# An encoder layer's state-space phase as a software pipeline with TensorE's order written out

## The chip, the cores and the metric

The kernel runs on one core of a Trainium2 chip. The metric is the device time of one launch in microseconds (us), taken as the median of several runs. In the profile PE is TensorE (matmuls), PEld its weight loads, DVE VectorE, ACT ScalarE, POOL GpSimd, SP SyncE (which here only starts transfers).

## The reference

One layer of a hybrid encoder in fp32 over 1024 tokens of width 1024, followed by cross-attention into 256 memory rows and a squared-ReLU MLP. What matters here is the first sublayer, the state-space branch above all:

```python
h = rmsnorm(x, norm_mix); proj = h @ w_in                   # q, k, v, z, xBC, dt, two gates
attn = windowed_gqa_sink(q, k, v, sink)                     # 16 heads, 4 kv heads, |t-s| <= 128
xbc = silu(depthwise_conv_centred(xbc, conv_w, conv_b))     # 5 taps; 2048 x, 1024 B, 1024 C
dt  = softplus(dt_raw + dt_bias)                            # per direction and head
# per direction (the backward one on flipped tokens), per group of 4 heads, chunks of 128 tokens:
#   CB     = C @ B.T;  Wd = CB * exp(masked difference of cumulated dt*A)
#   y_diag = Wd @ (x*dt);  states = B.T @ (decay * x*dt)
#   prev   = running sum of states over the chunks, decayed
#   y_off  = (C @ prev) * exp(cumulated dt*A)
y = (y_fwd + y_bwd + d_skip * x) * silu(z); y = grouped_rmsnorm(y) * norm_g
merged = sigmoid(gate_a) * (attn @ w_attn_branch) + sigmoid(gate_b) * (y @ w_ssd_branch)
x = x + merged @ w_out                                      # then cross-attention, then the MLP
```

## The kernel before

Every matmul with a weight is done on exact high and low halves, in three matmuls (`mm3`, L79 on). A weight block of 128x1024 comes by SP's queue into one of 2 `raw` buffers, ScalarE makes its high half (`whi`, L67), GpSimd its low half (`wlo`, L68), in one of 3 slots. All activations of the layer stand in `hT` (in the trace `kt`), feature by feature, two halves of 512 tokens.

The phases follow each other: norms, memory keys and values and the decay sums of dt (`phase0`, `dt_part`, tiles `dtt`, `r`, `acc`, `e`), then `ssd_phase`, `attn_phase` (4 key/value heads), `merge_cross_phase`, `mlp_phase`.

`ssd_phase` loops over 8 groups. For a group: four conv tiles (two of x, tile `cx`; B, tile `cB`; C, tile `cC`), each 48 matmuls of 128x512 into a psum tile `cps` and then one ScalarE and four VectorE products for the five taps, a tanh and a product; transposes into token-major `xtok` and `btok` (`tm`); eight states (`st`, from `xs` = x times decay, and `btok`) and their running sum `prev`; the z projection, 192 matmuls of 128x256 (`zp`), into `zs`; the scan of eight chunks from the last to the first: rows of the cumulated decay loaded by ScalarE's queue, exponents `ef` and `eb`, `cb` = C @ B.T, the product of both with `xtok` (written `cb` too, L427), `yo` = C @ prev, the sum `y` in `yz`, its square sum; after each half of the chunks the scaling, the transposes `yt`, their eviction into `yts` and a store to `d_y`. Behind each group stands one gate tile of 48 matmuls (`gps`; two behind the last), its tanh `gt` stored for the merge. Attention has one gate tile behind each key/value head, the merge three at its start; their first matmuls are pinned in program order.

Nothing sets the order inside the phases but the scheduler: it lists each engine's instructions by its own estimates, within what buffers allow. psum is split into `pg` (2 tiles of 128x1024, for `cps` and `gps`) and `pp` (4 tiles of 128x512 for all else). The gates are dealt out by three tables:

```python
SSD_GATES = ((0,), (1,), (2,), (3,), (4,), (5,), (6,), (7, 8))
ATT_GATES = ((9,), (10,), (11,), (12,))
END_GATES = (13, 14, 15)
```

Of the kernel before, what the change touches and what calls it, by code (L numbers as in the profile page):

```python
# [60 lines left out]
def split_in(kx, src, hi, lo, eng=None):  # L61
    """Load src and split it: hi + lo == src exactly."""
    nc = kx.nc
    n = hi.shape[-1]
    raw = kx.wp.tile([P, 1024], F32, tag="raw", bufs=kx.raw_bufs, name="raw")[:, :n]
    nc.sync.dma_start(raw, src)
    nc.scalar.activation(hi, raw, AF.Copy)  # L67
    (eng or nc.gpsimd).tensor_tensor(lo, raw, hi.bitcast(F32), ALU.subtract)  # L68
# [10 lines left out]
def mm3(kx, out, l, r, first, last):  # L79
    """out += l.T @ r with l, r given as exact (hi, lo) pairs."""  # L80
    mm = kx.nc.tensor.matmul
    i = mm(out, l[0], r[0], start=first, stop=False)  # L82
# [3 lines left out]
    mm(out, l[0], r[1], start=False, stop=False)  # L86
    mm(out, l[1], r[0], start=False, stop=last)  # L87
# [17 lines left out]
def gemm_fm(kx, ps, w, act, first=True, last=True):  # L105
    """feature-major GEMM over one half of the tokens: ps = w.T @ act"""
# [25 lines left out]
def norm_tile(kx, pool, xt, xn, grow, dst, off):  # L132
    """RMSNorm of 128 rows, transposed and split into dst at token offset off."""
# [77 lines left out]
def dt_part(kx, ins, dr, p0):  # L211
    """Softplus of dt, the decay sums and their layouts; rows are (direction, half, head)."""
# [99 lines left out]
def ssd_phase(kx, ins, dr):  # L312
    nc, tc = kx.nc, kx.tc
    V, A, G, PE = nc.vector, nc.scalar, nc.gpsimd, nc.tensor
    with tc.tile_pool(name="p1", bufs=1) as sp:
# [4 lines left out]
        def conv_tile(g, i, tag, bufs):  # L320
            w = wload(kx, ins["wssd"][g, i])
            ps = kx.pg.tile([P, S], F32, tag="g", name="cps")
            for h in range(2):
                gemm_fm(kx, ps[:, h * 512:(h + 1) * 512], w, kx.hT[h])
            j = 4 * g + i
            cw = lambda k: kx.cw[:, 5 * j + k:5 * j + k + 1]
            acc = ca.tile([P, S], F32, tag=tag, bufs=bufs, name=tag)
# [7 lines left out]
            th = ca.tile([P, S], F32, tag="tab", bufs=1, name="th")  # L335
            A.activation(th, acc, AF.Tanh)
            V.scalar_tensor_tensor(acc, th, 1.0, acc, ALU.add, ALU.mult)
            return acc
# [9 lines left out]
        for g in range(NG):  # L348
            xtok = ca.tile([P, NT, 256], F32, tag="xtok", bufs=1, name="xtok")
            btok = ca.tile([P, NT, P], F32, tag="btok", bufs=1, name="btok")  # L350
            for i in range(2):
                tok_major(conv_tile(g, i, "cx", 2), xtok[:, :, i * P:(i + 1) * P])
            BT = conv_tile(g, 2, "cB", 2)
            tok_major(BT, btok)
            CT = conv_tile(g, 3, "cC", 1)

            hs = slice(4 * g, 4 * g + 4)
            prev = sp.tile([P, NT, 2, 256], F32, tag="prev", bufs=1, name="prev")

            def decay(d, c):  # L360
                o = 64 * d + 32 * (c // 4) + 4 * g
                return kx.dec[:, o:o + 4, c % 4:c % 4 + 1].broadcast_to([P, 4, 64])

            def heads(ap):
                return ap.rearrange("p (h q) -> p h q", h=4)

            for c in range(NT):
                xs = sp.tile([P, 2, 4, 64], F32, tag="xs", bufs=2, name="xs")
                V.tensor_tensor(xs, heads(xtok[:, c]).unsqueeze(1).broadcast_to([P, 2, 4, 64]),
                                kx.coef[:, c // 4, c % 4, :, hs].unsqueeze(3).broadcast_to([P, 2, 4, 64]), ALU.mult)  # L370
                lo, hi = (256 if c == NT - 1 else 0), (256 if c == 0 else 512)
                st = kx.pp.tile([P, 512], F32, tag="p", name="st")
                PE.matmul(st[:, lo:hi], btok[:, c], xs.rearrange("p d h q -> p (d h q)")[:, lo:hi],  # L373
                          start=True, stop=True)
                if c == 0:
                    A.activation(prev[:, 1, 0], st[:, :256], AF.Copy)
                elif c < NT - 1:
                    V.tensor_tensor(heads(prev[:, c + 1, 0]), heads(prev[:, c, 0]), decay(0, c), ALU.mult)
                    V.tensor_tensor(prev[:, c + 1, 0], prev[:, c + 1, 0], st[:, :256], ALU.add)
                if c > 0:  # L380
                    A.activation(prev[:, c - 1, 1], st[:, 256:], AF.Copy)
            for c in range(NT - 2, 0, -1):
                t = sp.tile([P, 256], F32, tag="p1", bufs=2, name="cb_t")
                G.tensor_tensor(heads(t), heads(prev[:, c, 1]), decay(1, c), ALU.mult)
                G.tensor_tensor(prev[:, c - 1, 1], prev[:, c - 1, 1], t, ALU.add)

            zhl = [sp.tile([P, 1024], F32R, tag=f"z{i}", bufs=1, name=f"z{i}") for i in range(2)]
            zw = [wload(kx, ins["wssd"][g, 4], hi=zhl[0], lo=zhl[1]), wload(kx, ins["wssd"][g, 5])]
            zws = wsplit(zw[0], 4) + wsplit(zw[1], 4)
            zs = sp.tile([P, NT, 256], F32, tag="zs", bufs=1, name="zs")  # L390
            for b in range(3, -1, -1):
                zp = kx.pp.tile([P, 512], F32, tag="p", name="zp")
                for j in range(2):
                    t = 2 * b + j
                    for k in range(NK):
                        mm3(kx, zp[:, j * 256:(j + 1) * 256],
                            act_pair(kx.hT[t // 4], k, slice((t % 4) * P, (t % 4) * P + P)),
                            zws[k], k == 0, k == NK - 1)
                zb = zs[:, 2 * b:2 * b + 2].rearrange("p c q -> p (c q)")
                A.activation(zb, zp, AF.Tanh, scale=0.5)  # L400
                V.scalar_tensor_tensor(zb, zb, 1.0, zp, ALU.add, ALU.mult)

            for b in (1, 0):
                yz = sp.tile([P, 4, 256], F32, tag="yz", bufs=1, name="yz")
                ss = sp.tile([P, 4], F32, tag="ss", bufs=2, name="ss")
                for j in range(3, -1, -1):
                    c = 4 * b + j
                    cl = slice(c * P, (c + 1) * P)
                    rows = sp.tile([P, 2, 4, P], F32, tag="rows", bufs=2, name="rows")
                    for d in range(2):  # L410
                        o = 64 * d + 32 * b + 4 * g
                        nc.scalar.dma_start(rows[:, d], dr.cs[o:o + 4, j * P:(j + 1) * P].partition_broadcast(P))
                    G.affine_select(out=rows[:, 0], in_=rows[:, 0], compare_op=ALU.is_ge, fill=NEG, base=0,
                                    pattern=[[0, 4], [1, P]], channel_multiplier=-1)
# [10 lines left out]
                    V.tensor_tensor(ef, ef, cb[:, :P].unsqueeze(1).broadcast_to([P, 4, P]), ALU.mult)
                    for h in range(4):
                        PE.matmul(cb[:, 256 + 64 * h:256 + 64 * h + 64], ef[:, h], xtok[:, c, 64 * h:64 * h + 64],  # L427
                                  start=True, stop=True)
                    lo, hi = (256 if c == 0 else 0), (256 if c == NT - 1 else 512)
                    yo = kx.pp.tile([P, 512], F32, tag="p", name="yo")  # L430
                    PE.matmul(yo[:, lo:hi], CT[:, cl], prev[:, c].rearrange("p d q -> p (d q)")[:, lo:hi],
                              start=True, stop=True)
                    d0, d1 = lo // 256, hi // 256
                    t = sp.tile([P, 2, 256], F32, tag="t", bufs=1, name="t")
# [23 lines left out]
            for m in SSD_GATES[g]:  # L458
                gate_block(kx, ins, dr, m, ca)
# [509 lines left out]
```

## Time and profile before

| what | us |
|---|---|
| median of 3 runs | 2534.68 (2529.97 to 2538.14) |
| profiled execution, its span | 2540.5 (no time of its own beside the span is given) |
| TensorE busy | 2446.7 |
| phase 0 | 0 to 59.9 |
| state-space phase | 59.9 to 979.9 |
| attention | 980 to about 1319 |
| merge and cross-attention | to about 1500 |
| MLP | to the end |

Rows of waits read "engine, waiting tile and line <- engine, tile and line waited for: total, times, longest". Rows of a timeline give start, length, engine, line, operation, tiles, shape and count, and in brackets the idle time before with what ended it. Rows of windows give the stretch, its length, and then busy time and instructions of PE, PEld, DVE, ACT and POOL, the granted clock of TensorE, the share of the DMA engines and GB/s.

### The profile page before, as it was taken

How to read it: one execution, taken by the hardware profiler on the slowest of the kernel's cores; microseconds unless marked ns; L12 is line 12 of the kernel's file. 1: busy time of each engine (PE TensorE's matmuls, PEld its weight loads, DVE VectorE, ACT ScalarE, POOL GpSimd, SP SyncE). 2: the span in 40 equal slices, each digit the busy share in tenths (PEclk: the TensorE clock that was granted, in tenths of full speed). 3: DMA queues.
4: the chain of work that ended last, by engine and by line, in shares of the span. 5: the costliest groups of instructions: out<-in, count | busy, mean ns of one | idle time of the engine just before them, and what ended most of it. 6: DMA issues, size and time to landing. Idle time of an engine off the chain costs nothing.

```text
span 2540.5 us, 32272 instructions
## 1 busy us (share of the span) xinstructions
PE 2446.7 (96%) x12348; PEld 2014.4 (79%) x12348; DVE 1286.9 (51%) x2033; ACT 1030.6 (41%) x2114; POOL 936.2 (37%) x808
## 2 busy tenths in 40 slices
PE   7899999999999999999999999999999999999998
PEld 6677877777787778777778878888988888888887
DVE  5856556565755655465553342335543434343435
ACT  5445436363544534576773232235432121212112
POOL 4253434344344433444454444224332131312120
PEclk9999999999999999999999999999999999999999
DMA  6223223131313312111125454412121121111111
GB/s 221 75 71 104 92 59 117 52 123 46 112 63 88 108 44 90 48 48 46 50 90 201 134 206 129 170 50 67 59 75 67 34 67 34 66 34 58 42 34 67
DMA packets 135914, 212.20 MB, mean 84 GB/s; under 512 B 9680, under 2 KB 84560, under 8 KB 135760
## 3 DMA queue, kind: packets, MB, share of 16 engines
q1 hardware_dynamic: 58528, 159.80, 18.9%
q10 hardware_dynamic: 77232, 50.35, 6.7%
q8 instruction: 97, 1.59, 0.3%
q14 instruction: 57, 0.47, 0.1%
HBM read 183.63 MB, written 26.48 MB: 83 GB/s over the span
## 4 chain that ended last, share of the span: by engine, by line
PE 71%; DVE 12%; ACT 6%; POOL 4%; DMA 3%; issue 3%; ACTq 0%; POOLq 0%; SPq 0%; DVEq 0%
PE dps L87 4%; PE dps L86 4%; PE dps L82 4%; PE ups L82 4%; PE ups L86 4%; PE ups L87 4%; PE mps L87 3%; PE mps L82 3%; PE mps L86 3%; PE zp L82 2%; PE zp L87 2%; PE zp L86 2%; DMA rows<-d_cs 2%; PE st L373 2%; PE gps L82 2%
## 5 line engine op out<-in xcount | busy, mean ns | idle before, releaser
L68 POOL TENSOR_TENSOR wlo<-raw,whi 128x1024 fp32r<-128x1024 f32 x170 | 416.6, 2452 | 570.4 <-ACT whi L67 556.4
L67 ACT ACTIVATE whi<-raw 128x1024 fp32r<-128x1024 f32 x172 | 181.8, 1057 | 365.0 <-PE mps L86 111.7
L850 DVE TENSOR_TENSOR x<-x,dps 128x512 f32<-128x512 f32 x256 | 175.6, 686 | 124.9 <-PE dps L87 123.2
L68 POOL TENSOR_TENSOR wdl<-raw,wdh 128x1024 fp32r<-128x1024 f32 x32 | 76.0, 2396 | 423.2 <-ACT wdh L67 423.2
L82 PE MATMUL cps<-kt,whi 128*128 128x512 f32 x512 | 203.0, 396 | 6.9 <-DVE cx L334 6.9
L86 PE MATMUL cps<-kt,whi 128*128 128x512 f32 x512 | 203.8, 398 | 0.0
L87 PE MATMUL cps<-kt,wlo 128*128 128x512 f32 x512 | 201.4, 393 | 0.0
L82 PE MATMUL ups<-kt,whi 128*128 128x512 f32 x512 | 199.7, 390 | 0.2
L86 PE MATMUL ups<-kt,whi 128*128 128x512 f32 x512 | 199.4, 390 | 0.0
L87 PE MATMUL ups<-kt,wlo 128*128 128x512 f32 x512 | 199.2, 389 | 0.0
L86 PE MATMUL dps<-wdl,u 128*128 128x512 f32 x512 | 199.2, 389 | 0.0
L87 PE MATMUL dps<-wdh,u 128*128 128x512 f32 x512 | 199.2, 389 | 0.0
L82 PE MATMUL dps<-wdh,u 128*128 128x512 f32 x512 | 199.2, 389 | 0.0
L824 DVE TENSOR_TENSOR u<-ups,ru 128x512 f32<-128x512 f32 x64 | 44.1, 689 | 256.5 <-ACT ru L822 254.3
L67 ACT ACTIVATE wdh<-raw 128x1024 fp32r<-128x1024 f32 x32 | 32.3, 1053 | 229.9 <-PE dps L87 229.7
L82 PEld LDWEIGHTS cps<-kt,whi 128*128 128x128 f32 x512 | 96.6, 189 | 27.1 <-issue 7.7
L82 PEld LDWEIGHTS ups<-kt,whi 128*128 128x128 f32 x512 | 96.1, 188 | 20.7 <-DVE u L824 0.6
L86 PEld LDWEIGHTS ups<-kt,whi 128*128 128x128 f32 x512 | 96.1, 188 | 20.0 <-DVE kt L145 0.2
L87 PEld LDWEIGHTS ups<-kt,wlo 128*128 128x128 f32 x512 | 96.1, 188 | 20.0
L87 PEld LDWEIGHTS dps<-wdh,u 128*128 128x128 f32 x512 | 96.1, 188 | 20.0
L82 PEld LDWEIGHTS dps<-wdh,u 128*128 128x128 f32 x512 | 96.1, 188 | 20.0
L86 PEld LDWEIGHTS dps<-wdl,u 128*128 128x128 f32 x512 | 96.1, 188 | 19.9
(311 smaller groups left out, 6460.2 us busy)
## 6 DMA issues: line engine op xcount, KB each, us to landing
rows<-d_cs ACTq DMA_DIRECT2D x128, 256.0 KB, 3.8
raw<-in_wssd_dram SPq DMA_DIRECT2D x48, 512.0 KB, 3.9
raw<-in_wsb_dram SPq DMA_DIRECT2D x32, 512.0 KB, 3.3
raw<-in_wup_dram SPq DMA_DIRECT2D x32, 512.0 KB, 3.2
raw<-in_wdn_dram SPq DMA_DIRECT2D x32, 512.0 KB, 3.2
x<-in_x_dram SPq DMA_DIRECT2D x16, 512.0 KB, 7.7
raw<-in_wg_dram SPq DMA_DIRECT2D x16, 512.0 KB, 3.9
raw<-in_wa_dram SPq DMA_DIRECT2D x16, 512.0 KB, 3.3
```

Source lines behind the costliest of these rows:

```text
L67: nc.scalar.activation(hi, raw, AF.Copy)
L68: (eng or nc.gpsimd).tensor_tensor(lo, raw, hi.bitcast(F32), ALU.subtract)
L82: i = mm(out, l[0], r[0], start=first, stop=False)
L86: mm(out, l[0], r[1], start=False, stop=False)
L87: mm(out, l[1], r[0], start=False, stop=last)
L373: PE.matmul(st[:, lo:hi], btok[:, c], xs.rearrange("p d h q -> p (d h q)")[:, lo:hi], start=True, stop=True)
L824: V.tensor_tensor(u2, pv, r, ALU.mult)
L850: V.tensor_tensor(xh, xh, ps, ALU.add)
```

## The change

`ssd_phase` is written as a list of jobs, under a manual schedule for TensorE: in it TensorE's instructions run in the order of the code; the other engines stay with the scheduler. A job loads the next job's weights, then runs its matmuls in chunks of three (one `mm3`), and after given chunks other work is dealt in. For group g the jobs are conv 0, conv 1, gate g, conv 2, conv 3, z. The scan steps of group g−1 stand after chunks 8 and 16 of the first four; a step issues the next chunk's loads, exponents and `cb` (`prep`), then its own products. The group's states stand after every eighth chunk of z. In group 0 conv 0 and conv 1 alternate by halves, and nothing is dealt into them. At the end gates 8, 9 and 10 take the last group's steps. So 11 gates stand in the phase, three in attention (none for the last key/value head), two in the merge. Buffers: `cB` 2 to 1, `tab` (tanh and gate) 1 to 2, `yz` one of 128x4x256 to six of 128x256; the square goes into `zs`. Gate and y stores go on SP's queue.

```diff
-SSD_GATES = ((0,), (1,), (2,), (3,), (4,), (5,), (6,), (7, 8))
-ATT_GATES = ((9,), (10,), (11,), (12,))
-END_GATES = (13, 14, 15)
+ATT_GATES = ((11,), (12,), (13,), ())
+END_GATES = (14, 15)
...
-    with tc.tile_pool(name="p1", bufs=1) as sp:
+    with tc.tile_pool(name="p1", bufs=1) as sp, tc.manual_schedule(engines={mybir.EngineType.PE}):
...
+        def first_job(q):
...
+            def run(ws):
+                pss = [psum_g("cps") for _ in range(2)]
+                for h in range(2):
+                    for i in range(2):
+                        yield from fm_chunks(pss[i], ws[i], (h,))
+                for i in range(2):
+                    conv_post(q, i, pss[i])
...
+        def gate_job(m):
...
+                gt = ca.tile([P, 2, 512], F32, tag="tab", bufs=2, name="gt")
+                for h in range(2):
+                    A.activation(gt[:, h], ps[:, h * 512:(h + 1) * 512], AF.Tanh, scale=0.5)
+                    nc.sync.dma_start(dr.gt[m][h], gt[:, h])
...
-                yz = sp.tile([P, 4, 256], F32, tag="yz", bufs=1, name="yz")
+            y = q.yz[j] = sp.tile([P, 256], F32, tag="yz", bufs=6, name="yz")
...
-                    A.activation(jk2 := sp.tile([P, 256], F32, tag="jk2", bufs=1, name="jk2"), y, AF.Square,
-                                 accum_out=ss[:, j:j + 1])
+            A.activation(q.zs[:, c], y, AF.Square, accum_out=q.ss[:, j:j + 1])
...
-                    (nc.sync if g == NG - 1 else nc.scalar).dma_start(dr.y[g][b][:, f], yo_s)
+                nc.sync.dma_start(dr.y[q.g][b][:, f], yo_s)
...
+            if g == 0:
+                job(first_job(q), {})
+                job(gate_job(0), {})
+                job(conv_job(q, 2), {})
+                job(conv_job(q, 3), {8: [(tm_x, q)]})
+            else:
+                job(conv_job(q, 0), {8: [(step, o, 7)], 16: [(step, o, 6)]})
+                job(conv_job(q, 1), {8: [(step, o, 5)], 16: [(step, o, 4)]})
+                job(gate_job(g), {8: [(step, o, 3)], 16: [(step, o, 2), (yt, o)]})
+                job(conv_job(q, 2), {8: [(step, o, 1)], 16: [(step, o, 0)]})
+                job(conv_job(q, 3), {8: [(tm_x, q)], 16: [(yt, o)]})
+            at = {8 * c + 8: [(state, q, c)] for c in range(NT)}
+            at[2] = [(tm_b, q)]
+            at[64] += [(back, q), (prep, q, 7)]
+            job(z_job(q), at)
+        q = gs[7]
+        job(gate_job(8), {5: [(step, q, 7)], 10: [(step, q, 6)], 16: [(step, q, 5)]})
+        job(gate_job(9), {5: [(step, q, 4)], 10: [(step, q, 3)], 16: [(step, q, 2), (yt, q)]})
+        job(gate_job(10), {5: [(step, q, 1)], 10: [(step, q, 0)]})
+        w = jobs[0][0][0]()
+        for n, ((_, run), at) in enumerate(jobs):
+            nxt = jobs[n + 1][0][0]() if n + 1 < len(jobs) else None
+            i = 0
+            for _ in run(w):
+                i += 1
+                for f, *a in at.get(i, ()):
+                    f(*a)
+            w = nxt
+        yt(q)
```

In the code after, the three lines of `mm3` are L81, L85 and L86 instead of L82, L86 and L87.

The first place is group 0 on VectorE, at the end of the dt chain (`u`, `e`, `acc`, `r`, `cs`). Before:

```order
L332 SCALAR_TENSOR_TENSOR cx<-cps,cols,cx 128x1022
L254 SCALAR_TENSOR_TENSOR acc<-acc,w_720 128x512
L334 SCALAR_TENSOR_TENSOR cx<-cps,cols,cx 128x1022
L254 SCALAR_TENSOR_TENSOR acc<-acc,w_720 128x512 x2
L337 SCALAR_TENSOR_TENSOR cx<-th,cx 128x1024
L254 SCALAR_TENSOR_TENSOR acc<-acc,w_720 128x512
L256 SCALAR_TENSOR_TENSOR acc<-acc,r 128x512
L260 TENSOR_SCALAR mk<-u 128x512
L257 TENSOR_TENSOR e<-e,acc 128x512
```

and its COPY_PREDICATED followed five rows on. After, from that row:

```order
L260 COPY_PREDICATED acc<-mk,e 128x512
L349 SCALAR_TENSOR_TENSOR cx<-cps,cols,cx 128x1023
L262 SCALAR_TENSOR_TENSOR acc<-u,acc 128x512
L351 SCALAR_TENSOR_TENSOR cx<-cps,cols,cx 128x1023
L263 TENSOR_SCALAR u<-e,ea 128x512
L349 SCALAR_TENSOR_TENSOR cx<-cps,cols,cx 128x1022
L270 SCALAR_TENSOR_TENSOR cs<-r,u 64x512
L271 SCALAR_TENSOR_TENSOR cs<-r,u 64x512
L275 COPY end<-cs 64x4
L351 SCALAR_TENSOR_TENSOR cx<-cps,cols,cx 128x1022
L276 COPY end<-cs 64x4
```

The products of conv 0 (the first four `cx<-cps` rows) stood between the rows of L254, ahead of COPY_PREDICATED; now the first of them stands behind it. On TensorE meanwhile, where the `cps` of conv 3 stood around dt's transposes (`dtt`), gate 0 stands now. Before:

```order
L82 MATMUL cps<-kt,whi 128x512
L86 MATMUL cps<-kt,whi 128x512
L290 MATMUL dtt<-ident,r 128x128 x4
L290 MATMUL dtt<-ident,acc 128x128 x4
L290 MATMUL dtt<-ident,e 128x128 x4
L345 MATMUL tm<-ident,cx 128x128 x16
L87 MATMUL cps<-kt,wlo 128x512
L82 MATMUL cps<-kt,whi 128x512
```

After:

```order
L86 MATMUL gps<-kt,wlo 128x512
L81 MATMUL gps<-kt,whi 128x512
L85 MATMUL gps<-kt,whi 128x512
L289 MATMUL dtt<-ident,r 128x128 x4
L289 MATMUL dtt<-ident,acc 128x128 x4
L289 MATMUL dtt<-ident,e 128x128 x4
L86 MATMUL gps<-kt,wlo 128x512
L81 MATMUL gps<-kt,whi 128x512
```

The `dtt` transposes come eleven matmuls into gate 0 instead of in conv 3, and the `tm` of x no longer follow them.

The second place is TensorE at the end of a group's scan half. Before, in group 1's conv tiles:

```order
L86 MATMUL cps<-kt,whi 128x512
L454 MATMUL yt<-ident,yz 128x128 x2
L418 MATMUL cb<-cC,cB 128x128
L454 MATMUL yt<-ident,yz 128x128 x4
L431 MATMUL yo<-prev,cC 128x512
L454 MATMUL yt<-ident,yz 128x128 x2
L427 MATMUL cb<-xtok,ef 128x64 x4
L87 MATMUL cps<-kt,wlo 128x512
L82 MATMUL cps<-kt,whi 128x512
L86 MATMUL cps<-kt,whi 128x512
L418 MATMUL cb<-cC,cB 128x128
```

After, at the end of gate 1 (the last step of the half, then its transposes):

```order
L86 MATMUL gps<-kt,wlo 128x512
L479 MATMUL cb<-cC,cB 128x128
L499 MATMUL cb<-xtok,ef 128x64 x4
L503 MATMUL yo<-prev,cC 128x512
L530 MATMUL yt<-ident,yz 128x128 x8
L81 MATMUL cps<-kt,whi 128x512
L85 MATMUL cps<-kt,whi 128x512
```

The transposes `yt` were cut up among other chunks' products; now a step is one block, and `yt` follows it in one piece. The states stood together amid or behind a few gate matmuls (before, the last of group 1):

```order
L82 MATMUL gps<-kt,whi 128x512
L86 MATMUL gps<-kt,whi 128x512
L373 MATMUL st<-xs,btok 128x512 x2
L373 MATMUL st<-xs,btok 128x256
L82 MATMUL zp<-z_2169,kt 128x256
L86 MATMUL zp<-z_2170,kt 128x256
```

After (the first of group 0):

```order
L85 MATMUL zp<-wlo,kt 128x256
L86 MATMUL zp<-whi,kt 128x256
L450 MATMUL st<-xs,btok 128x256
L81 MATMUL zp<-z_1060,kt 128x256
L85 MATMUL zp<-z_1061,kt 128x256
```

Each state now stands alone between z's matmuls, 24 of them from one to the next.

The third place is TensorE in attention's last key/value head (`qps` the queries, `sps` scores, `pt` transposes of the weights, `op` outputs). Before:

```order
L87 MATMUL qps<-kt,wlo 128x512
L545 MATMUL sps<-kh,q 128x256
L546 MATMUL sps<-kl,q 128x256
L545 MATMUL sps<-kh,q 128x256
L546 MATMUL sps<-kl,q 128x256
L82 MATMUL gps<-kt,whi 128x512
L86 MATMUL gps<-kt,whi 128x512
L87 MATMUL gps<-kt,wlo 128x512
```

After, some rows into it:

```order
L658 MATMUL sps<-kl,q 128x384
L657 MATMUL sps<-kh,q 128x384
L658 MATMUL sps<-kl,q 128x384
L680 MATMUL pt<-ident,t_11757 128x128 x8
L689 MATMUL op<-ph,vhl 128x512
L657 MATMUL sps<-kh,q 128x384
L658 MATMUL sps<-kl,q 128x384
L690 MATMUL op<-pl,vhl 128x512
L657 MATMUL sps<-kh,q 128x384
```

Before, gate matmuls stood between the scores; now scores, transposes and outputs follow each other directly, and the gate matmuls of the merge come behind the last output.

More of the change, by code (lines that the diff above doesn't have):

```diff
@@ L318, in ssd_phase, with heads, fm_chunks, conv_post @@
         nc.sync.dma_start(dsk, ins["dskip"].partition_broadcast(P))
[L320 to L325, printed above, removed]
+        def heads(ap):
+            return ap.rearrange("p (h q) -> p h q", h=4)
+        class Group:
+            pass
+        gs = []
+        for g in range(NG):
+            q = Group()
+            q.g, q.hs, q.cx = g, slice(4 * g, 4 * g + 4), []
+            gs.append(q)
+        def fm_chunks(ps, w, halves=(0, 1)):
+            ws = wsplit(w)
+            for h in halves:
+                for k in range(NK):
+                    mm3(kx, ps[:, h * 512:(h + 1) * 512], ws[k], act_pair(kx.hT[h], k), k == 0, k == NK - 1)
+                    yield
+        def conv_post(q, i, ps):
+            tag = ("cx", "cx", "cB", "cC")[i]
+            j = 4 * q.g + i
             cw = lambda k: kx.cw[:, 5 * j + k:5 * j + k + 1]
-            acc = ca.tile([P, S], F32, tag=tag, bufs=bufs, name=tag)
+            acc = ca.tile([P, S], F32, tag=tag, bufs=2 if i < 2 else 1, name=tag)
             A.activation(acc, ps, AF.Identity, bias=kx.cb[:, j:j + 1], scale=cw(2))
@@ new lines, in psum_g, with conv_job, load, run @@
+        def psum_g(name):
+            return kx.pg.tile([P, S], F32, tag="g", name=name)
+        def conv_job(q, i):
+            def load():
+                return wload(kx, ins["wssd"][q.g, i])
+            def run(w):
+                ps = psum_g("cps")
+                yield from fm_chunks(ps, w)
+                conv_post(q, i, ps)
+            return load, run
+        def first_job(q):
+            def load():
+                return [wload(kx, ins["wssd"][q.g, i]) for i in range(2)]
+            def run(ws):
[5 more added lines that the diff above has]
+                    conv_post(q, i, pss[i])
+            return load, run
@@ new lines, in gate_job, with load, run @@
+        def gate_job(m):
+            def load():
+                return wload(kx, ins["wg"][m])
+            def run(w):
+                ps = psum_g("gps")
+                yield from fm_chunks(ps, w)
+                gt = ca.tile([P, 2, 512], F32, tag="tab", bufs=2, name="gt")
+                for h in range(2):
+                    A.activation(gt[:, h], ps[:, h * 512:(h + 1) * 512], AF.Tanh, scale=0.5)
+                    nc.sync.dma_start(dr.gt[m][h], gt[:, h])
+            return load, run
@@ L346, in tok_major, with tm_x @@
                 A.activation(dst[:, 4 * b:4 * b + 4], pt.rearrange("p (c j) -> p c j", c=4), AF.Copy)
-        for g in range(NG):
-            xtok = ca.tile([P, NT, 256], F32, tag="xtok", bufs=1, name="xtok")
-            btok = ca.tile([P, NT, P], F32, tag="btok", bufs=1, name="btok")
+        def tm_x(q):
+            q.xtok = ca.tile([P, NT, 256], F32, tag="xtok", bufs=1, name="xtok")
             for i in range(2):
[L352 to L381, printed above, removed]
@@ L382, in ssd_phase, with back @@
+        def back(q):
+            prev = q.prev
             for c in range(NT - 2, 0, -1):
                 t = sp.tile([P, 256], F32, tag="p1", bufs=2, name="cb_t")
[L384 removed]
+                G.tensor_tensor(heads(t), heads(prev[:, c, 1]), decay(q, 1, c), ALU.mult)
                 G.tensor_tensor(prev[:, c - 1, 1], prev[:, c - 1, 1], t, ALU.add)
[L387 removed]
@@ L388, in ssd_phase @@
[L388 to L401, printed above, removed]
@@ new lines, in yt @@
+        def yt(q):
+            b, yz = q.done
+            for f in range(2):
+                pt = kx.pp.tile([P, 512], F32, tag="p", name="yt")
+                for j in range(4):
+                    PE.transpose(pt[:, j * P:(j + 1) * P], yz[j][:, f * P:(f + 1) * P], kx.ident)
+                yo_s = sp.tile([P, 512], F32, tag="yts", bufs=1, name="yts")
+                A.activation(yo_s, pt, AF.Copy, scale=kx.g_ssd[:, 2 * q.g + f:2 * q.g + f + 1])
+                nc.sync.dma_start(dr.y[q.g][b][:, f], yo_s)
```

162 lines of the change are left out of this document (108 added, 54 removed).

## The prediction

> **What bounds the kernel.** I read the page of the profile first, then busy time by stage, then TensorE's waits inside the state-space stage.
>
> ```profile
> PE 2446.7 (96%) x12348; PEld 2014.4 (79%) x12348; DVE 1286.9 (51%) x2033; ACT 1030.6 (41%) x2114; POOL 936.2 (37%) x808
> 59.93:979.90 919.97, 861.96 (x4724) 702.57 (x4723) 577.80 (x783) 443.79 (x1028) 398.03 (x408) 0.99 0.28 84
> PE yt L454 <- ACT yz L450: 18.8, 16, 2.3
> PE st L373 <- DVE xs L369: 13.4, 8, 1.9
> PE tm L345 <- DVE cx L337: 8.3, 13, 1.6
> PE tm L345 <- DVE cB L337: 8.2, 7, 1.6
> PE cps L82 <- DVE cx L334: 6.9, 2, 5.0
> PE st L373 <- ACT btok L346: 2.6, 2, 2.3
> PE cb L427 <- DVE ef L425: 1.2, 1, 1.2
> PE yo L431 <- ACT yts L456: 0.4, 1, 0.4
> ```
>
> TensorE is the bound: 96% busy, 93.8 us idle in a span of 2540.5. The state-space stage (59.93 to 979.90) holds 919.97 − 861.96 = 58.0 us of that idle, and the list of waits from 60 to 1030 says where: 59.8 us in all, of which 6.9 is the start (cps) and 52.9 recurs group by group (yt, st, tm, cb, yo). The most that a better order inside this stage can give is about 58 us, plus what the idle costs afterwards in clock.
>
> It costs that in three groups. Windows behind their last states (length, TensorE busy, then other engines; the third number from the right is the granted clock), and one of the matmuls in them:
>
> ```profile
> 235.00:240.00 5.00, 4.84 (x13) 3.54 (x14) 5.00 (x8) 0.38 (x1) 0.00 (x0) 0.66 0.32 105
> 345.00:349.00 4.00, 4.00 (x6) 1.42 (x6) 2.21 (x2) 2.72 (x4) 2.34 (x1) 0.57 0.15 60
> 461.00:465.00 4.00, 3.85 (x8) 2.54 (x9) 4.00 (x6) 0.38 (x1) 0.00 (x0) 0.57 0.41 131
> 573.00:578.00 5.00, 3.11 (x11) 1.80 (x10) 5.00 (x5) 0.73 (x2) 1.79 (x1) 1.00 0.33 108
> 461.15 1.68 PE L373 MATMUL st<-xs,btok 128*128 128x512 f32 x2 [1.88 <-DVE xs L369]
> ```
>
> (1 − clock) × length is 1.7 us in each, 5.1 in the three; the window from 573 is a group with the same wait of 1.9 us and no such stretch.
>
> The Trainium skill (TensorE: Matmul & The Clock Gate, "What's actually happening") says that the clock is halved after an idle window of about 3.4 us whose phase runs freely. The halved stretches agree; gaps of 1.9 us suffice here, in three groups and not in others, which the free phase would allow.
>
> **What the change does, part by part.** The same matmuls run; what differs is where they stand. TensorE's switches between weight matmuls and other matmuls are 153 in the stage before and 153 after, counted in the two orders, so I price switching at 0.
>
> *Waits of the groups.* The state matmuls (st) now stand 8 chunks of z apart, the transposes tm and yt stand at least two chunks after what they need, a step's products cb stand a half conv after its exponents. Two rows of a dealt-in block of before give the pace of a step, 0.94 each for yo and the four cb (406.81 − 405.87, and as much again), 2.0 with the small cb:
>
> ```profile
> 405.87 1.02 PE L431 MATMUL yo<-prev,cC 128*128 128x512 f32 x2
> 406.81 1.10 PE L427 MATMUL cb<-xtok,ef 128*128 128x64 f32 x8
> ```
>
> Eight chunks of a conv are 24 matmuls of 0.228, 5.5 us. By hand, with z's end as zero, steps so fall at 6, 13, 20, 28, 35, 43, 52, 59 (a yt with its transposes ahead of the seventh), conv 3 ends at 75, B's transposes at 78, the first state at 82, and what each needs is there 2 to 4 us sooner. So all 52.9 go, and the 5.1 of half clock with them, −58.0. Cover for each is the projection it is dealt into. What is late next: ScalarE's queue, below. Residue: in the trace the smallest wait of a dealt-in product is yo's 0.4; one such in each of 7.5 groups is +3 (ends 0 and one of 1.2, as for cb, in each: 9). The last yt, behind gate 10, has nothing dealt around it: +1 (a yt wait averages 18.8 / 16 = 1.2).
>
> *Start.* Before, conv 2 (at 83.76) and conv 3 (at 99.88) waited for psum that VectorE's conv products release:
>
> ```profile
> 81.24 0.39 PE L86 MATMUL cps<-kt,whi 128*128 128x512 f32 x1
> 81.47 0.39 PE L87 MATMUL cps<-kt,wlo 128*128 128x512 f32 x1
> 83.76 0.47 PE L82 MATMUL cps<-kt,whi 128*128 128x512 f32 x1 [1.91 <-DVE cx L334]
> 99.88 0.77 PE L82 MATMUL cps<-kt,whi 128*128 128x512 f32 x1 [4.96 <-DVE cx L334]
> 99.88:103.30 3.42, 3.42 (x8) 0.52 0.11 38
> 106.73 0.60 PE L290 MATMUL dtt<-ident,r 128*128 128x128 f32 x4
> 76.96 1.28 DVE L332 SCALAR_TENSOR_TENSOR cx<-cps,cols,cx 128x1023 f32<-128x1023 f32 x1
> 84.86 1.22 DVE L337 SCALAR_TENSOR_TENSOR cx<-th,cx 128x1024 f32<-128x1024 f32 x1
> 91.78 0.75 DVE L261 COPY_PREDICATED acc<-mk,e 128x512 f32<-128x512 int32 x1
> 99.65 1.20 DVE L271 TENSOR_TENSOR_SCAN cs<-r,u 64x512 f32<-64x512 f32 x1
> ```
>
> Now conv 0 and 1 are interleaved by halves and gate 0 follows, and in VectorE's order all of conv 0's products stand behind the dt chain's COPY_PREDICATED. That ended at 92.5 with five conv instructions of about 1.25 ahead of it (76.96 to 84.86), so it now ends near 86.3; then come four conv products (1.2 apart), two short operations, two scans (1.2 each) and a small copy: 8.7, so psum is free at 95.0. TensorE has run dry at 81.7: a wait of 13.3 for gate 0 against 1.91 + 4.96 = 6.9, +6.4. Ends: +2.6 if the slow VectorE instructions beside GpSimd's fall elsewhere (a wait of 9.5), +8 (15). The half-rate stretch behind the wait (3.42 us at 0.52) comes once as before: 0.
>
> *Group 0.* The exponents of its first step and the loads of its rows now stand on ScalarE ahead of the next projection's work. Loads take 3.8 to land and eight exponents about 0.5 each (rows below, and the 128x256 exponent): up to 7.8; I take +3, nearer to zero, since a conv of 10.9 us stands over it.
>
> *Stores.* 42 gate and y stores leave ScalarE's queue for SP's, behind weight loads. SP only waits; a y store that lands late holds the single yts buffer:
>
> ```profile
> rows<-d_cs ACTq DMA_DIRECT2D x128, 256.0 KB, 3.8
> d_y<-yts ACTq DMA_DIRECT2D x28, 256.0 KB, 2.4
> raw<-in_wssd_dram SPq DMA_DIRECT2D x48, 512.0 KB, 3.9
> L68 POOL TENSOR_TENSOR wlo<-raw,whi 128x1024 fp32r<-128x1024 f32 x170 | 416.6, 2452 | 570.4 <-ACT whi L67 556.4
> ```
>
> The second yt's eviction waits 2.4 for the first's store; in my hand timing this ends a microsecond before the first state needs ScalarE's btok. Priced 0 (ends −1, a ScalarE freed of issuing, and the rival below).
>
> *Gates.* Two more gates run in the stage, two fewer behind it: 0 in themselves. But attention's last key/value head loses its filler:
>
> ```profile
> 1257.78 0.28 PE L545 MATMUL sps<-kh,q 128*128 128x256 f32 x1
> 1265.21 0.51 ACT L553 ACTIVATE t<-t,nm 128x256 f32<-128x256 f32 x1 [3.04 <-DVE nm L549]
> 1317.05 0.42 PE L578 MATMUL op<-pl,vhl 128*128 128x512 f32 x1
> 1264.00:1318.00 54.00, 52.66 (x271) 40.63 (x270) 35.77 (x112) 42.83 (x114) 28.62 (x40) 1.00 0.13 38
> L553 ACT ACTIVATE t<-t,nm 128x384 f32<-128x384 f32 x24 | 14.4, 604 | 0.0
> L553 ACT ACTIVATE t<-t,nm 128x256 f32<-128x256 f32 x8 | 4.0, 496 | 3.0 <-DVE nm L549 3.0
> L571 ACT ACTIVATE ph<-pt 128x512 fp32r<-128x512 f32 x22 | 12.2, 594 | 3.6 <-PE pt L568 3.3
> L582 ACT ACTIVATE ob<-op 64x512 f32<-64x512 f32 x8 | 4.8, 594 | 0.2
> L581 ACT ACTIVATE oa<-op 64x512 f32<-64x512 f32 x8 | 4.7, 588 | 5.2 <-PE op L578 5.2
> ```
>
> From the first score to the last op it took 59.5 us with 100 gate matmuls among them; matmuls of this size stand 0.228 apart (81.24 and 81.47 above), so 22.8 of it was filler. Now none is there: TensorE runs scores, transposes and outputs alone, and the gates come behind. If the stretch shrinks by 22.8, nothing is lost. It can't: the first exponent comes 7.4 us in, and ScalarE then has 14.4 + 4.0 + 12.2 + 4.8 + 4.7 = 40.1, less some 2 that overlap in its pipeline: 45.5 at least, a shrink of 14 and a loss of 9. If it hardly shrinks (1.2), the loss is 21.5. In the window ScalarE was busy 42.83 of 54.00 with filler in TensorE's way; I let half of its 11.2 idle stay: 9 + 5.6 = 14.6, and call it +15.
>
> *Sum:* −52.9 − 5.1 + 3 + 1 + 6.4 + 3 + 0 + 15 = −29.6 us against the profiled execution's span. Its own 2540.5 is 5.8 over the median of the three runs (2534.68, 2529.97 to 2538.14); the difference carries over: 2505.
>
> **Rivals.**
> - *The head without filler loses nothing* (scores, exponents and outputs overlap better when no gate stands between): for it, ScalarE's idle was mostly waits for TensorE (3.3 and 5.2 in the rows); against it, the start of 7.4 alone has TensorE with nothing to do. −44.6: 2490. 12%.
> - *The waits move rather than go.* VectorE and ScalarE still carry the same work per group, and waits for them return at other places. If half of 52.9 and of 5.1 stays: −29.6 + 29 = −0.6: 2534. Against it: 577.80 and 443.79 busy of 919.97, so both have room. 10%.
> - *Slower: ScalarE's queue blocks behind yts.* Its order is fixed; the second yts waits for a store that stands on SP behind a weight load, which waits until GpSimd has released a raw buffer (2.45 us an instruction, 570.4 us idle for want of ScalarE's whi). Whatever stands behind on ScalarE (btok, the hi halves of the next weights) waits too, and TensorE for it. The gain of 29.6 is lost when this costs 29.6 / 7 = 4.2 us in each of seven groups, and it is slower by over 0.3% from 5.3; one GpSimd turn (2.45) and a landing weight load (3.9) would do it: 6.3 × 7 = 44, 2549. For it: one buffer, and four y stores a group. Against it: the loads run one job ahead. 8%.
>
> The Trainium skill (TensorE: Matmul & The Clock Gate, "Architectural detail") has ScalarE and VectorE as strict first-in-first-out queues. That is what this rival needs; the trace of before shows no instruction of theirs passing another, but can't show this wait.
>
> **Numbers.** The forecast has 70%, the rivals 12, 10 and 8. Its own range, with kv's loss from 9 to 21.5 and the start, group 0 and residue at their ends, is 2490 to 2525; the rest of the range is given to the first rival's edge: 2491 to 2526. A difference of 0.3% (7.6 us) is about what can be told from no change: faster below 2527, which forecast, first rival and a third of the second give (85%); the rest of the second is the same (7%), the third slower (8%).
>
> **What the changed profile would show.** Right: in the groups no TensorE wait for xs, cB, cx or yz over 1 us, groups about 107 us apart instead of 113, and a granted clock of 1.00 behind the states; one wait of 10 to 15 us before the first gps; no gps from attention's last qps to its last op, with TensorE idle about 15 there and that stretch some 52 us long. Wrong: waits for ScalarE's btok, yts or whi in every group (third rival), or a last head of 37 us (first). What would make me wrong unseen is TensorE falling to half clock through the last head, where it works only about two thirds of the time: its 36 us of matmuls would then take longer than ScalarE's 38.

## The result, and the profile after

The change made the kernel slower by a little: 2542.93 us (median of 20 runs, 2537.56 to 2548.03) against 2538.18 for 20 runs of the kernel before, a ratio of 1.0022 [1.0013, 1.0031]. The 4.8 us are clear of the noise, but less than the 7.6 that the forecast counted as no change; the forecast was 2505. The two profiled executions are as good as equal in span, 2540.7 after and 2540.5 before. The granted clock over the whole kernel is lower in every run after: 0.984 to 0.989 in the 20, against 0.993 to 0.998 in the runs of the kernel before that were made beside the experiments. First the page's line of busy times, then TensorE's waits from 59 to 1030 after:

```profile
PE 2446.7 (96%) x12348; PEld 2035.1 (80%) x12348; DVE 1241.4 (49%) x2033; ACT 1024.6 (40%) x2114; POOL 934.5 (37%) x808
PE yt L530 <- DVE t L507: 27.9, 8, 3.7
PE gps L81 <- DVE cx L351: 12.6, 1, 12.6
PE tm L426 <- DVE cB L354: 4.7, 4, 2.1
PE tm L426 <- ACT yts L532: 2.3, 4, 1.0
PE yt L530 <- ACT yz L522: 0.2, 1, 0.2
```

Every kind of wait that the forecast wanted gone is gone or small, and the one at the start has nearly the size foretold. But the first row is new: eight times, once for each group's scan, the transposes yt wait 3.5 us on average for VectorE's `t` (`yo` times the cumulated decay, which reads `yo` out of psum).

The window rows from the first conv to the first query show the stage, before and after:

```profile
59.93:1017.62 957.69, 897.36 (x4974) 735.56 (x4973) 589.39 (x792) 459.90 (x1054) 405.43 (x415) 0.99 0.27 83
```

```profile
59.68:1020.74 961.06, 912.97 (x5070) 770.40 (x5068) 539.29 (x792) 456.88 (x1060) 411.18 (x417) 0.98 0.27 84
```

It became 3.4 us longer with two more gates in it (96 matmuls, 21.8 us): a gain of 18.5. Then the last head. Before and after, the last query matmul, the last output, the first matmul of the merge and the first of the MLP:

```profile
1257.55 0.40 PE L87 MATMUL qps<-kt,wlo 128*128 128x512 f32 x1
...
1317.05 0.42 PE L578 MATMUL op<-pl,vhl 128*128 128x512 f32 x1
...
1338.20 0.40 PE L82 MATMUL mps<-at,whi 128*128 128x512 f32 x1
...
1830.82 0.47 PE L82 MATMUL ups<-kt,whi 128*128 128x512 f32 x1
```

```profile
1260.83 0.40 PE L86 MATMUL qps<-kt,wlo 128*128 128x512 f32 x1
...
1321.69 0.50 PE L690 MATMUL op<-pl,vhl 128*128 128x512 f32 x1 [0.23 <-DVE pl L684]
...
1343.83 0.40 PE L81 MATMUL mps<-at,whi 128*128 128x512 f32 x1
...
1831.30 0.47 PE L81 MATMUL ups<-kt,whi 128*128 128x512 f32 x1
```

From the last query to the merge: 80.65 before, 83.00 after with two gates fewer, a loss of 83.00 − 80.65 + 21.8 = 24.2. From the merge to the MLP: 492.62 and 487.47, 5.2 gained. The kernel before has a wait of 4.2 for GpSimd there, with half clock behind it; the profiled execution after doesn't. Half of the fourteen experiments' profiles have this wait (3.2 to 4.8), half don't. There is one profile of each kernel, so whether the wait comes with the kernel or with the execution isn't known. −18.5 + 24.2 − 5.2, and no more than 0.3 in each other stretch, gives the equal spans of the profiles. Between the medians of 20 runs stand 4.8 us: the median after is 2.2 over its profiled span, the one before 2.3 under.

### The profile page after: what moved, and what is told of

The parts are those of the page before. It is cut to its first block, busy times and chain, and to the rows that moved or that the text cites. A ratio compares the mean times of both kernels' runs of the same rounds, so it can differ in the third digit from the quotient of the medians.

```text
span 2540.7 us, 32190 instructions
## 1 busy us (share of the span) xinstructions
PE 2446.7 (96%) x12348; PEld 2035.1 (80%) x12348; DVE 1241.4 (49%) x2033; ACT 1024.6 (40%) x2114; POOL 934.5 (37%) x808
## 4 chain that ended last, share of the span: by engine, by line
PE 74%; POOL 7%; DVE 6%; ACT 5%; DMA 4%; issue 3%; POOLq 0%; SPq 0%; ACTq 0%; DVEq 0%
PE ups L81 5%; PE ups L86 5%; PE ups L85 5%; PE dps L86 4%; PE dps L81 4%; PE dps L85 4%; PE mps L85 3%; PE mps L86 3%; PE mps L81 3%; DMA rows<-d_cs 3%; PE zp L86 2%; PE zp L85 2%; PE zp L81 2%; PE cps L81 2%; PE cps L85 2%
## 5 line engine op out<-in xcount | busy, mean ns | idle before, releaser
L81 PE MATMUL cps<-kt,whi 128*128 128x512 f32 x512 | 217.0, 424 | 0.0
L86 PE MATMUL cps<-kt,wlo 128*128 128x512 f32 x512 | 202.6, 396 | 0.0
L85 PE MATMUL cps<-kt,whi 128*128 128x512 f32 x512 | 202.5, 395 | 0.0
L81 PE MATMUL ups<-kt,whi 128*128 128x512 f32 x512 | 199.7, 390 | 0.0
L85 PE MATMUL ups<-kt,whi 128*128 128x512 f32 x512 | 199.4, 390 | 0.0
L86 PE MATMUL ups<-kt,wlo 128*128 128x512 f32 x512 | 199.2, 389 | 0.0
L81 PE MATMUL dps<-wdh,u 128*128 128x512 f32 x512 | 199.2, 389 | 0.0
L85 PE MATMUL dps<-wdl,u 128*128 128x512 f32 x512 | 199.2, 389 | 0.0
L86 PE MATMUL dps<-wdh,u 128*128 128x512 f32 x512 | 199.2, 389 | 0.0
L81 PE MATMUL gps<-kt,whi 128*128 128x512 f32 x256 | 109.7, 429 | 12.6 <-DVE cx L351 12.6
L85 PEld LDWEIGHTS cps<-kt,whi 128*128 128x128 f32 x512 | 98.6, 193 | 24.2 <-issue 5.0
L81 PEld LDWEIGHTS cps<-kt,whi 128*128 128x128 f32 x512 | 98.6, 193 | 24.0 <-issue 5.0
L86 PEld LDWEIGHTS cps<-kt,wlo 128*128 128x128 f32 x512 | 98.1, 192 | 21.7
L464 POOL TENSOR_TENSOR cb_t<-prev,dec 128x256 f32<-128x256 f32 x48 | 32.2, 672 | 224.8 <-ACT prev L458 222.2
L81 PEld LDWEIGHTS ups<-kt,whi 128*128 128x128 f32 x512 | 96.1, 188 | 20.4 <-ACT kt L143 0.3
L85 PEld LDWEIGHTS ups<-kt,whi 128*128 128x128 f32 x512 | 96.1, 188 | 20.0 <-DVE kt L144 0.2
```

The source lines that it names most:

```text
L464: G.tensor_tensor(heads(t), heads(prev[:, c, 1]), decay(q, 1, c), ALU.mult)
```

## The experiments

Times are given as ratios to runs of the kernel before on the same chip; 0.001 is 2.5 us. The changed kernel stands at 1.0022.

**1. The new wait.** Here it is in group 3, TensorE and VectorE after, and the windows behind this wait and behind group 5's:

```profile
425.01 1.08 PE L503 MATMUL yo<-prev,cC 128*128 128x512 f32 x2
425.92 0.67 PE L530 MATMUL yt<-ident,yz 128*128 128x128 f32 x4
430.26 1.11 PE L530 MATMUL yt<-ident,yz 128*128 128x128 f32 x4 [3.67 <-DVE t L507]
```

```profile
427.19 1.23 DVE L354 SCALAR_TENSOR_TENSOR cx<-th,cx 128x1024 f32<-128x1024 f32 x1 [0.53 <-ACT th L353]
428.33 0.68 DVE L486 TENSOR_TENSOR ef<-ef,eb 128x512 f32<-128x512 f32 x1
428.93 0.68 DVE L487 TENSOR_TENSOR ef<-ef,cb 128x512 f32<-128x512 f32 x1
429.53 0.68 DVE L507 TENSOR_TENSOR t<-yo,ecs 128x512 f32<-128x512 f32 x1
```

```profile
430.00:436.00 6.00, 5.74 (x16) 4.72 (x17) 2.50 (x5) 3.17 (x9) 5.43 (x5) 0.52 0.80 246
651.00:658.00 7.00, 6.22 (x18) 5.07 (x19) 3.02 (x6) 4.01 (x12) 5.56 (x5) 0.53 0.80 249
```

The second yt of a half needs a psum tile, and the one that comes free is yo's, just written by the step that yt follows. VectorE's `t` frees it, and in VectorE's order a conv's tanh product (held up by ScalarE's tanh) and both operations on `ef` stand ahead of it. Then TensorE runs at half clock for most of the next 6 us. The first edit takes yt away from that place:

```diff
-                job(gate_job(g), {8: [(step, o, 3)], 16: [(step, o, 2), (yt, o)]})
-                job(conv_job(q, 2), {8: [(step, o, 1)], 16: [(step, o, 0)]})
+                job(gate_job(g), {8: [(step, o, 3)], 16: [(step, o, 2)]})
+                job(conv_job(q, 2), {4: [(yt, o)], 8: [(step, o, 1)], 16: [(step, o, 0)]})
...
-        job(gate_job(9), {5: [(step, q, 4)], 10: [(step, q, 3)], 16: [(step, q, 2), (yt, q)]})
-        job(gate_job(10), {5: [(step, q, 1)], 10: [(step, q, 0)]})
+        job(gate_job(9), {5: [(step, q, 4)], 10: [(step, q, 3)], 16: [(step, q, 2)]})
+        job(gate_job(10), {2: [(yt, q)], 5: [(step, q, 1)], 10: [(step, q, 0)]})
```

> The changed kernel with one edit: the transposes yt of a group's first half stand after chunk 4 of the next job instead of straight behind the step whose psum they need. Theory (the groups' gain was eaten by the wait of the second yt block for psum, 27.9 us in eight, and by the half-clock stretches that follow it, some 15 us): yt <- DVE t falls below 5 us in all, the half-clock stretches of the groups mostly go, and the kernel takes 30 to 43 us less than the changed one, about 2505. Rival (VectorE and ScalarE can't feed the groups faster, any wait taken away comes back elsewhere): other waits of some 25 us appear in the groups, 2535 to 2543.

Ratio 0.9988 [0.9979, 0.9997]: 9 us less than the changed kernel, not 30 to 43. The waits from 59 to 1030:

```profile
PE yo L503 <- ACT yts L532: 13.9, 7, 2.0
PE gps L81 <- DVE cx L351: 12.6, 1, 12.6
PE tm L426 <- ACT yts L532: 10.3, 7, 2.2
PE yt L530 <- DVE t L507: 9.2, 8, 1.8
```

Of the 27.9, 9.2 stayed at yt, while the waits for yts at yo and tm rose from 2.3 to 24.2, so 30 became 33: the rival in effect, the wait moved to what needs psum next. The 9 us themselves aren't found in this profile, which is of the slowest of the eleven runs (2547.43): its stage took 960.5, where the changed kernel's took 961.1.

**2. The last head.** `ATT_GATES = ((10,), (11,), (12,), (13,))`, and the end of the state-space phase is

```diff
+        job(gate_job(8), {4: [(step, q, 7)], 8: [(step, q, 6)], 12: [(step, q, 5)], 16: [(step, q, 4)]})
+        job(gate_job(9), {4: [(step, q, 3)], 8: [(step, q, 2)], 10: [(yt, q)], 12: [(step, q, 1)], 16: [(step, q, 0)]})
```

> The changed kernel with gate 10 moved from the end of the state-space phase to attention, so that every key/value head has a gate again, and the last scan's eight steps dealt into two gates instead of three. Theory (the last head without filler cost about 24 us, not 15, because TensorE also falls to half clock there): 20 to 25 us less than the changed kernel, about 2520, with no half clock between the last queries and the last output. The forecast's own price: 15 less, 2528. Rival (the eight steps are now too dense at the end, and the loss only moves): 2535 to 2543.

Ratio 0.9968 [0.9956, 0.9979], 14 us less than the changed kernel: short of the theory's 20 to 25, near the forecast's own price of 15. But the head itself gave nearly all 24 back, as the theory said. Its window here, and the changed kernel's, where the granted clock is 0.86 and TensorE is idle for 16 us:

```profile
1252.00:1311.50 59.50, 58.16 (x298) 44.87 (x297) 39.46 (x120) 45.35 (x116) 31.01 (x41) 1.00 0.14 41
```

```profile
1260.00:1322.00 62.00, 46.00 (x202) 34.02 (x201) 36.86 (x120) 42.37 (x111) 28.54 (x40) 0.86 0.08 22
```

The changed kernel's largest wait there, from 1255 to 1322:

```profile
PE op L689 <- ACT ph L683: 5.7, 4, 3.1
```

From the last query to the merge it took 70.4 with one gate more than the changed kernel's 83.0, so 23.5 less like for like (a gate is 10.9). The denser steps at the end of the state-space phase took 2 of that back, and the stretch from merge to MLP was 493.8, 6.3 longer than in the changed kernel's profile. In it TensorE waits 2.8 us for `at`, the merge's first input, which the changed kernel's doesn't: behind the last output 44 gate matmuls stand here, 96 there. So the filler that one stage got was missing in the next.

**3. Both edits.**

> Both edits together. Theory: they add, 50 to 68 us less than the changed kernel, 2475 to 2493, faster than before by 2 to 2.5%. Rival (groups are bound by VectorE and ScalarE): 2515 to 2530.

Ratio 0.9954 [0.9942, 0.9966], 17 us under the changed kernel where the two alone had 9 and 14: they nearly add, but to far less than the 50 to 68 expected, since the first is so much smaller.

**4. The tables alone.** The kernel before with `SSD_GATES` ending in (7, 8, 9, 10), and the changed kernel's other two tables.

> The kernel before with the changed kernel's tables of gates alone: four gates behind the last group, none in the last key/value head, two at the merge; the scheduler still orders the groups. Theory: it loses what the last head loses, 20 to 25 us, about 2560, with half clock in that head. The forecast's price: 15, 2553. Rival (the loss in the last head comes from the pipeline, not from the missing gate): 2538.

Ratio 1.0088 [1.0072, 1.0105]: 22 us lost, by the tables of gates alone, with the old order in the groups. From the last query to the merge it took 82.3, which by the same count is a loss of 23.4. If tables and pipeline simply add, the pipeline proper gained 1.0088 − 1.0022, some 17 us, and the tables took it and 5 more.

**5. Two yts buffers.** To the first experiment, `yts` with `bufs=2`, `ef` with `bufs=2` instead of 3.

> The kernel of the first experiment (transposes yt in the next job) with two yts buffers instead of one; for the room ef has two instead of three. Theory (the wait moved from yt to what stands behind it, since the second yt keeps its psum tile until the first's store has left the only yts buffer): the waits of yo and tm for yts, 24 us in all, go, the half-clock stretches of the groups with them, and the kernel takes 2505 to 2518. Rival (four psum tiles are too few, whoever holds them): the same waits for other releasers, 2530 to 2540.

Ratio 0.9961 [0.9947, 0.9975], 2528: past the rival's range by 2 us, short of the theory's by 10. yo and tm still waited 4.0 and 7.6 for yts, and a wait of cb for `ef` had come, 12.7 us.

**6. Dealt in apart.** To the third, with `yt` taking the blocks that it is to do as an argument:

```diff
+                job(conv_job(q, 2), {4: [(yt, o, (0,))], 8: [(step, o, 1)], 12: [(yt, o, (1,))], 16: [(step, o, 0)]})
+                job(conv_job(q, 3), {8: [(tm_x, q)], 12: [(yt, o, (0,))], 16: [(yt, o, (1,))]})
```

> The third experiment's kernel (filler back, yt in the next job) with the two yt blocks of a half dealt in apart, after chunks 4 and 12 of conv 2 and 12 and 16 of conv 3; one yts buffer as before. Theory: no two of them meet in the one buffer any more, the waits for yts and for t (34 us in that kernel's profile) fall below 8, and it takes 2490 to 2503. Rival (VectorE and ScalarE bind the groups): 2520 to 2530.

Ratio 1.0041 [1.0027, 1.0054], 22 us slower than the third. The theory fell by its own edit: the waits for yts and t nearly went, and a larger one came, four chunks earlier being too early for the second half's yz:

```profile
PE yt L530 <- ACT yz L522: 36.6, 8, 5.7
PE gps L81 <- DVE cx L351: 12.6, 1, 12.6
PE tm L426 <- DVE yz L515: 6.0, 7, 1.8
```

**7. Gate 0 first.** To the sixth, in group 0 `gate_job(0)`, `conv_job(q, 0)`, `conv_job(q, 1)` instead of `first_job(q)`, `gate_job(0)`.

> As the sixth, and in group 0 gate 0 stands first and conv 0 and conv 1 follow one after the other, so that the psum tile that conv 1 takes is released by ScalarE and not by VectorE's conv products behind the dt chain. Theory: the wait of 12.6 us at the start shrinks to 2 to 5 and its half-clock stretch goes: 9 to 13 us less than the sixth. Rival (the dt chain itself is awaited by all that follows): the wait stands before conv 2 with the same length, no change.

Ratio 1.0007 [0.9997, 1.0017], 7 us less than the sixth by the medians and 9 by the ratios. The wait for psum went; 6.2 us are left, for the dt chain itself, before its transposes, over the 2 to 5 expected. The half clock that was to go is still there (0.50 from 97 to 101):

```profile
97.24 1.12 PE L289 MATMUL dtt<-ident,r 128*128 128x128 f32 x4 [6.18 <-DVE r L283]
```

**8. The scheduler's order.** The changed code without `tc.manual_schedule`.

> The changed kernel without the manual schedule: same code, buffers and gates, but the scheduler orders TensorE. The fourth experiment's kernel (old code, same gates) took 2564 and the changed one 2543, so the pipeline's rewriting gains some 21. Theory (the order written out makes that gain): 2555 to 2566. Rival (the code's placement and buffers make it, and the scheduler finds as good an order): 2540 to 2548.

Ratio 1.0086 [1.0069, 1.0102]: where the fourth stands, and in the theory's range: without the manual schedule the rewriting gains nothing over the fourth. But what the manual schedule changes is small. TensorE's order in this trace is the changed kernel's, matmul by matmul, but for one place in each of the eight scans, where two projection matmuls stand ahead of the second yt block. Here is the one that belongs to the rows of experiment 1:

```profile
432.16 0.94 PE L530 MATMUL yt<-ident,yz 128*128 128x128 f32 x4
432.86 0.48 PE L81 MATMUL cps<-kt,whi 128*128 128x512 f32 x1
433.18 0.40 PE L85 MATMUL cps<-kt,whi 128*128 128x512 f32 x1
436.79 0.69 PE L530 MATMUL yt<-ident,yz 128*128 128x128 f32 x4 [3.21 <-DVE t L507]
```

VectorE, ScalarE and GpSimd have a few instructions elsewhere too; on VectorE it is B's conv products, in seven groups. So the sequence of the code gives nearly the whole order on TensorE, with or without the manual schedule. These few moves make the stage 14.8 us longer (975.9 against 961.1), of which the lists of waits show 6.5. Which of the moves costs how much isn't known.

**9 and 10.** The ninth is the fifth with the filler and gate 0 first added; the tenth is the ninth with `p1 += t` of a step on VectorE instead of GpSimd.

> The three edits that helped, together: yt after chunk 4 of the next job with two yts buffers (2528), filler back for the last head, gate 0 first in group 0. Theory (they act at three different places and add: filler 10 to 15, gate first 7): 2504 to 2513. Rival (TensorE's waits for the other engines take part of it back): 2516 to 2525.

> As the ninth, with one addition of each step (p and t, 128x256) on VectorE instead of GpSimd. Theory (in the groups VectorE's yz stands behind GpSimd's p, which stands behind a weight block's wlo of 2.4 us; ScalarE's square and the eviction of yts stand behind yz, and TensorE behind that psum): VectorE's waits for p go, TensorE's for yts shrink by half, 4 to 12 us less than the ninth. Rival (another 0.4 us a step on VectorE delays the conv products as much): within 4 us of it, or slower.

Ninth: 0.9894 [0.9872, 0.9916], 2514.87, two us over the theory's range and one under the rival's. Tenth: 0.9869 [0.9849, 0.9889], 2509.70, 5 to 6 us less with intervals that overlap, and faster than the kernel before by 1.3%. VectorE's waits for the sum on GpSimd, 20.7 us in the ninth's profile, are gone. So are the five half-clock stretches that the ninth has in the groups (two at the tail stand in both), and the granted clock is 0.994 to 0.996 in the tenth's runs where it is 0.992 to 0.994 in the ninth's. TensorE's waits for yts did not shrink (8.7 and 8.5 at tm), so the way it helped isn't the one foretold; why the clock held isn't shown.

**11 to 13. Which buffer.** The changed kernel with two yts and two ef buffers; with two ef buffers alone; with two yts, three ef and one eb.

> The changed kernel with two yts buffers (and two of ef) and the transposes yt where the change put them. Theory (the second yt waits there for the psum tile of yo, which VectorE's t releases, not for yts): yt <- DVE t stays near 28 us, 2535 to 2543. Rival (the one yts buffer is what holds the groups): 2520 to 2530.

> The changed kernel with ef's three buffers cut to two and nothing else. Theory (the second yt waits because, in VectorE's order, the sum of the next chunk's exponents stands straight ahead of t and waits for ScalarE; with two ef buffers that sum stands four instructions earlier): yt <- DVE t falls from 28 us to under 8 and the kernel takes what the eleventh took, a ratio to before of 0.995 to 1.000. Rival (the second yts buffer did it): yt <- DVE t stays near 28, ratio 1.001 to 1.004.

> The changed kernel with two yts buffers and ef's three; the room comes from eb, one buffer instead of two. In VectorE's order the sum of exponents stands straight ahead of t, as in the changed kernel. Theory: yt <- DVE t stays above 20 us, ratio to before 1.000 to 1.006. Rival (two yts buffers free psum earlier): under 8, ratio 0.995 to 0.999.

Ratios 0.9978 [0.9965, 0.9991], 0.9980 [0.9967, 0.9993] and 1.0103 [1.0090, 1.0116]. In the eleventh yt's wait for `t` fell to 4.4, against the theory; the twelfth shows why. The twelfth's waits, then the thirteenth's first row and VectorE there, in group 3:

```profile
PE gps L81 <- DVE cx L351: 12.6, 1, 12.6
PE cb L499 <- DVE ef L487: 12.4, 8, 2.0
PE tm L426 <- ACT yts L532: 9.2, 7, 1.8
PE yt L530 <- DVE t L507: 3.7, 3, 3.0
```

```profile
PE yt L530 <- DVE t L507: 24.8, 8, 3.2
437.28 0.69 DVE L486 TENSOR_TENSOR ef<-ef,eb 128x512 f32<-128x512 f32 x1 [2.72 <-ACT eb L485]
437.89 0.68 DVE L487 TENSOR_TENSOR ef<-ef,cb 128x512 f32<-128x512 f32 x1
438.49 0.68 DVE L507 TENSOR_TENSOR t<-yo,ecs 128x512 f32<-128x512 f32 x1
```

Two ef buffers alone take the wait away (27.9 to 3.7), and the second yts buffer of the eleventh adds nothing to that. TensorE's order is the changed kernel's in both, the twelfth and the thirteenth. VectorE's order at that place, changed kernel first, then the twelfth:

```
L354 SCALAR_TENSOR_TENSOR cx<-th,cx 128x1024
L486 TENSOR_TENSOR ef<-ef,eb 128x512
L487 TENSOR_TENSOR ef<-ef,cb 128x512
L507 TENSOR_TENSOR t<-yo,ecs 128x512
```

```
L486 TENSOR_TENSOR ef<-ef,eb 128x512
L516 TENSOR_TENSOR yz<-yz,p_2830 128x256
L517 TENSOR_TENSOR yz<-yz,zs 128x256
L487 TENSOR_TENSOR ef<-ef,cb 128x512
L507 TENSOR_TENSOR t<-yo,ecs 128x512
```

With two buffers the scheduler puts the conv's tanh product and the sum of exponents further ahead, and `t` comes soon after yo. The price is the wait of cb for ef (12.4). The gain is 11 us, 1.0022 to 0.9980. The thirteenth doesn't test the second yts buffer: its single eb is an edit of its own. The sum of exponents stands ahead of `t` there too, but now waits 2.7 us for ScalarE to write eb (47.2 us in all such waits in the stage, 13.8 in the changed kernel).

**14.** The tenth with three ef buffers and one eb.

> The tenth experiment's kernel with three ef buffers and one of eb. Theory (two ef buffers give the wait of cb for ef, 17 us there, since a chunk's exponents can't be written before the chunk two ahead of it is through): cb <- DVE ef falls below 8 us, but ef's sum stands ahead of t again; with yt in the next job that costs little, and it takes 3 to 10 us less than the tenth. Rival (the wait is for VectorE's work, whatever the buffers): no change, or slower through the single eb.

Ratio 1.0033 [1.0020, 1.0046]: the wait of cb for ef fell to 2.1 as expected, but yt's for `t` was back with 24.5, and the kernel 42 us slower than the tenth. As in the thirteenth, the sum ahead of `t` waits for the single eb (46.2 us in the stage, 2.3 in the tenth), the rival's "slower through the single eb", so three ef buffers by themselves were not tested. It does show that moving yt to the next job doesn't help when VectorE comes to `t` late.

## Why the prediction was wrong

The forecast was −29.6 in span; the profiles differ by +0.2. Of the 29.8 between them the stage makes 26.1 (−44.6 forecast, −18.5 measured) and the last head 9.2, less the 5.2 from merge to MLP and 0.3 elsewhere. In the median it is 38: the forecast put it 5.8 under the profiled span, and it came out 2.2 over. By its terms:

- *"So all 52.9 go, and the 5.1 of half clock with them"*: the step that failed. The recurring waits named went from 53 to 7, but 28 stands in a new one, and half clock rose from 5.1 to some 17 in the groups (one minus the clock, added up over seven stretches, six of them behind yt's new wait). The groups came 109.5 apart where 107 was foretold, and 113 before. The hand timing checked that each operand was ready; it took VectorE as free when asked and didn't follow who frees the psum tile of a transposed block. Experiment 12 shows that VectorE's order decides it: TensorE's order is the same, and the wait is 3.7.
- *Switches priced at 0*: the work does not stay the same. From each row's start to the next, less waits, st took 47.5 before and 27.5 after, yo 46.1 and 32.6, z 184.1 and 207.5: what st gained, z lost. The stage without its waits rose by 15.4, which is −6.4 net of two gates. Half clock while TensorE worked, the start included, cost 6.7 before and 15.8 after, so with that set aside the stage's own work fell by 15.5 us, which no term foresaw. Experiment 8 has the same 27.5 and 32.6, so it isn't the manual schedule; what it is, no run tells. The stage's −18.5 is −12.1 of waits (59.8 to 47.7), +9.1 of half clock and −15.5 of work.
- *Start*: right. 12.6 measured, 13.3 forecast; its half clock came once, as said (3.5 us behind the wait, clock 0.53). The small terms (+3, +1 and +3) are right in sum: 7.2 us of waits stand beside yt's and the start's, though nearly all at the transposes of B, where none was foretold.
- *Last head*: the mechanism was right and the size off. +15 forecast from 9 to 21.5, 24.2 in the profile, 22 by experiment 4. TensorE's idle came out at 16, where about 15 was foretold. The stretch took 60.9 instead of some 52, and the term that the sum left out is the half clock: 0.86 over 62 us, up to 8.7. The prediction's last sentence had named it.
- *Rivals*: the second, waits that move, is what happened (2534 given, 10%); in the changed kernel, and again in experiments 1, 5 and 6. The third was hardly seen: ScalarE waited 9.1 us in nine times for a y store to leave yts, and TensorE's tm behind it 2.3 in all. It did matter once yt stood elsewhere (24 us in experiment 1), through the one buffer and ScalarE's order: there, in group 3, SP issued the store as soon as its yts was written.

What the Trainium skill (TensorE: Matmul & The Clock Gate, "HAM oscillation — how this bites in real kernels") says of a stage that stops and starts, that the clock falls again and again, fits the last head, with four stretches at half clock. The page gives gaps of over 3.4 us as the limit; here the longest single wait is 3.1 (the row in experiment 2), so shorter ones in a row were enough.

## What to carry to other kernels

Writing out one engine's order fixes only that engine: the others keep an order made by other rules, and a wait written out of TensorE's list returns where it meets theirs. Before writing a list out, look at what the scheduler makes of the same code: here the two lists differed in one place for each scan, and the kernels by 16 us. When checking such a list by hand, follow for each block the psum tile that it takes, to the instruction that frees it and to what stands ahead of that on its engine; after a build, read that in the order. And work that fills another stage's waits has a value there: moving gates out of the last head cost 22 us without touching a group.

## What the runs showed of the hardware

A wait of 3.7 us could cost more than itself: behind the one in group 3 TensorE ran at 0.52 for 6 us, so its full price was about 3.7 + 6 × 0.48 = 6.6 us. It was not always so: of the eight waits for `t`, three were followed by half-clock stretches of 6.8 us, three by stretches of 3.4, as behind three waits of 1.9, 2.3 and 1.9 us before, and two by none. Half clock also followed where no single wait was over 3.1 us, in the last head (0.86 over 62 us with TensorE idle for 16). A buffer count off the critical path (ef, three to two) moved the time by 11 us, because the scheduler then ordered VectorE otherwise.
